# A third seven-product chunk in each feed-forward block, and the turned operand copied out of PSUM by ScalarE

## The chip, the core and the metric

The kernel runs on one core of a Trainium2 chip. The metric is device time in microseconds (us) of one execution: the median of three runs is 1015.85 us (1015.84 to 1016.21). Five engines take part: TensorE (PE in the rows; its weight loads are PEld), VectorE (DVE), ScalarE (ACT), GpSimd (POOL) and SyncE (SP, which issues the weights' transfers). In the trace each engine's own instructions run in the order in which the program lists them, and an instruction that waits holds up those behind it.

## What is computed

Two layers over 256 tokens of width 1024 in float32; each layer is feed-forward, mixer, feed-forward, and every part has a norm ahead of it and one behind it. Cut to what matters here:

```python
def swiglu(x, w_gate, w_up, w_down):
    return (jax.nn.silu(x @ w_gate) * (x @ w_up)) @ w_down

for l in range(2):
    h = swiglu(rms_norm(x, g[0, 0]), ffn_w_gate[l, 0], ffn_w_up[l, 0], ffn_w_down[l, 0])
    x = x + 0.5 * rms_norm(h, g[0, 1])
    ...                       # even_mixer for l = 0, odd_mixer for l = 1
    h = swiglu(rms_norm(x, g[2, 0]), ffn_w_gate[l, 1], ffn_w_up[l, 1], ffn_w_down[l, 1])
    x = x + 0.5 * rms_norm(h, g[2, 1])
```

The gate and up matrices are 1024 x 2816, the down matrix is 2816 x 1024. There are four feed-forward blocks in all.

## The kernel before

**Precision.** A float32 operand is kept as two fp32r tiles, a rounded one (`hi`) and the rest (`lo`), and a product is three matmuls: hi by hi, lo by hi, hi by lo (`mm3`, lines 294 to 296). Of every weight piece of 128 x 1024 ScalarE makes `whi` (line 269) and then VectorE makes `wlo` = raw - whi (line 274). A piece of a gate or up matrix holds two of the eight blocks of 128 rows for 512 columns.

**Buffers.** The raw pieces come over SyncE's queue, 512 KB each, into 13 buffers. The `whi`/`wlo` pairs go through nine buffers in turn (five of one pool and four of another, `RING`), so the cast of a piece can begin only when TensorE is done with the piece nine places before it. `fill` lists pieces up to seven ahead of the matmuls that use them.

**A feed-forward block** takes the 2816 columns in six chunks, `CHUNKS = [512, 512, 512, 256, 512, 512]`, and the two token tiles t = 0, 1. An ordinary chunk of 512 makes gate and up with 8 row blocks x 2 tokens x 2 matrices x 3 = 96 matmuls of 128x512. Then `silu` (ScalarE) and `gated` (VectorE, line 501) make h, which TensorE turns in the next chunk (`turn`, line 403) with a cast and a subtraction behind it (lines 410, 411). The down products of a chunk (48 matmuls for 512 columns) come one chunk later, those of the last two chunks at the block's end.

**A chunk with seven products.** `SEVEN = (2, 4)` names chunks (counted from 0) that are made as a 2x2 block product: the two token tiles by the upper and lower 512 rows on one side, those rows by gate and up on the other. It takes seven block products instead of eight (`seven`, lines 562 to 605), each over four row blocks: 7 x 4 x 3 = 84 matmuls. The price is paid by the other engines: seven pieces of two `whi`/`wlo` pairs instead of four, so 14 casts and 14 subtractions instead of 8 and 8; eight additions of raw pieces on VectorE (line 214); three copies of a PSUM bank to SBUF on ScalarE (`held`, line 572) and three additions on VectorE (`plus`, line 576). The products, in order, go into banks X, W, Y: X, [turn t=0], W, [turn t=1], X again (after the first `held`), Y, X again (after the second), [downs], X again (after the third), W again. The last `plus` needs the end of the last product; then `gated` makes h.

**The sums.** The seven products also need four sums of the token operand's quarters (`row_sums`, lines 523 to 548). Their inputs, the turned x times the norm's weights, are put together again from the `hi` and `lo` halves by four VectorE additions of 128x512 (line 531), and eight more VectorE operations follow.

**The order.** A scheduler in front of the program moves instructions within an engine's list by its own costs and priorities; what it made of the change is shown below.

Of the kernel before, what the change touches and what calls it, by code (L numbers as in the profile page):

```python
# [12 lines left out]
F32 = mybir.dt.float32  # L13
# [3 lines left out]
ALU = mybir.AluOpType  # L17
# [3 lines left out]
P = 128  # L21
# [15 lines left out]
SEVEN = (2, 4)  # L37
# [146 lines left out]
def forward(ctx, tc, a):  # L184
# [211 lines left out]
    def to_T(src, dst, n, j0=0, bank=bank):  # L396

        hi, lo = dst
        for b in range(0, n, 4):
            w = min(4, n - b)  # L400
            ps = bank()
            for i in range(w):
                nc.tensor.transpose(ps[:, i * P:(i + 1) * P], src[:, (b + i) * P:(b + i + 1) * P], ident)  # L403
            done = split(ps[:, :w * P], hi[:, j0 + b:j0 + b + w, :], lo[:, j0 + b:j0 + b + w, :])
        return done
# [7 lines left out]
    def turn_x(t, xg):  # L413

        def half(i):
            return lambda: to_T(xg[:, i * 512:(i + 1) * 512], xT[t], 4, 4 * i, ybank)
        return [half(0), half(1)]
# [35 lines left out]
    def finish(ys, gpost, half, gnext, pieces, at):  # L453


        xg = post_norm(0, ys[0], gpost, half, gnext)
        turns = turn_x(0, xg)
        for i, p in enumerate(pieces):
            if gnext is not None and i in at:
                turns[at.index(i)]()  # L460
            p()
        r0 = rms_x(0) if gnext is not None else None
        xg = post_norm(1, ys[1], gpost, half, gnext)
        if gnext is None:
            return None, None
        return [r0, rms_x(1)], turn_x(1, xg)
# [15 lines left out]
    def ffn(scope, r, turn1, gpost, gnext, at=None):  # L482
        fx, fp, fr = scope
        with fx:
# [38 lines left out]
            def row_sums(fp):  # L523

                xf = [cp.tile([P, D], F32, name="xf", tag="c") for _ in range(NT)]
                A = [[xf[t][:, 512 * i:512 * i + 512] for i in range(2)] for t in range(NT)]
                tt = nc.vector.tensor_tensor
                for t in range(NT):
                    for i in range(2):
                        hi, lo = (v.rearrange("p k n -> p (k n)").bitcast(F32) for v in half(t, i))  # L530
                        tt(A[t][i], hi, lo, op=ALU.add)
# [131 lines left out]
            out = finish(y, gpost, True, gnext, pieces, [n0, n0 + wl // 2])  # L663
# [59 lines left out]
    def mix_out():  # L723
# [21 lines left out]
        def second(gpost, gnext):  # L745
# [4 lines left out]
            return finish(y, gpost, False, gnext, pieces, [8, 10])  # L750
# [492 lines left out]
    def turn_first(t):  # L1243

        def half(i):
            def go():
# [5 lines left out]
                c = cp.tile([P, D], F32, name="c", tag="c")[:, 0:512]  # L1252
# [30 lines left out]
    r, turn1 = ffn(scope, r, turn1, load_g(0, 2, 1), load_g(1, 0, 0))  # L1283
# [34 lines left out]
```

## Time and profile before

| | |
|---|---|
| median of three runs | 1015.85 us |
| the profiled execution, whole | 1009.94 us |
| its span, first to last instruction | 1008.2 us |
| PE busy | 990.5 us (98%) |
| DVE busy | 788.4 us (78%) |
| ACT busy | 583.4 us (58%) |
| weights read | 182.35 MB |
| granted TensorE clock, mean | 1.000 |

The share of busy time is a mean over stretches that differ: where TensorE is never kept waiting, work on the other engines costs nothing, and where it is, the engine that it waits for sets the pace. Matmuls overlap in the pipeline, so that one shows 0.39 us while the next begins 0.227 us later; the pace is read from starts.

### The profile page before, as it was taken

How to read it: one execution, taken by the hardware profiler on the slowest of the kernel's cores; microseconds unless marked ns; L12 is line 12 of the kernel's file. 1: busy time of each engine (PE TensorE's matmuls, PEld its weight loads, DVE VectorE, ACT ScalarE, POOL GpSimd, SP SyncE). 2: the span in 40 equal slices, each digit the busy share in tenths (PEclk: the TensorE clock that was granted, in tenths of full speed). 3: DMA queues.
4: the chain of work that ended last, by engine and by line, in shares of the span. 5: the costliest groups of instructions: out<-in, count | busy, mean ns of one | idle time of the engine just before them, and what ended most of it. 6: DMA issues, size and time to landing. Idle time of an engine off the chain costs nothing.

```text
span 1008.2 us, 13275 instructions
## 1 busy us (share of the span) xinstructions
PE 990.5 (98%) x4883; PEld 825.0 (82%) x4883; DVE 788.4 (78%) x1068; ACT 583.4 (58%) x846; POOL 52.2 (5%) x61
## 2 busy tenths in 40 slices
PE   8999999999999999999999999999999999999997
PEld 6888988888788888888888889888877788889886
DVE  5998996578567899888479988865776779988852
ACT  5746584377644755657447474744665657474731
POOL 1000000021202000000010000000010210000000
PEclk9999999999999999999999999999999999999999
DMA  8938273375223883827456392737634357292701
GB/s 349 374 113 295 70 255 116 105 260 184 99 69 119 312 288 104 305 68 266 175 200 233 113 306 80 271 117 259 230 125 137 119 171 244 95 304 85 252 1 42
DMA packets 51905, 184.26 MB, mean 183 GB/s; under 512 B 6136, under 2 KB 6528, under 8 KB 51840
## 3 DMA queue, kind: packets, MB, share of 16 engines
q1 hardware_dynamic: 48960, 176.05, 50.7%
q10 hardware_dynamic: 2880, 7.37, 2.2%
q8 instruction: 38, 0.62, 0.3%
q14 instruction: 27, 0.22, 0.1%
HBM read 182.35 MB, written 1.05 MB: 182 GB/s over the span
## 4 chain that ended last, share of the span: by engine, by line
PE 89%; DVE 5%; ACT 2%; issue 1%; POOL 1%; DMA 1%; SPq 0%; POOLq 0%; DVEq 0%; ACTq 0%
PE w L294 16%; PE w L296 16%; PE w L295 16%; PE y L294 9%; PE y L296 9%; PE y L295 9%; PE w L342 7%; DVE wlo L274 2%; PE w L403 2%; PE w L1023 1%; ACT whi L269 1%; PE y L403 1%; DMA raw<-in_w_dram 1%; POOL pm L1156 1%; DVE pm L1158 0%
## 5 line engine op out<-in xcount | busy, mean ns | idle before, releaser
L269 ACT CAST whi<-raw 128x1024 fp32r<-128x1024 f32 (+2 forms) x379 | 391.4, 1049 | 268.7 <-PE y L296 90.3
L274 DVE TENSOR_TENSOR wlo<-raw,whi 128x1024 fp32r<-128x1024 f32 (+2 forms) x379 | 456.7, 1228 | 96.1 <-ACT whi L269 92.4
L294 PE MATMUL w<-whi,xThi 128*128 128x512 f32 (+1 forms) x676 | 252.7, 374 | 0.0
L296 PE MATMUL w<-whi,xTlo 128*128 128x512 f32 (+1 forms) x676 | 249.7, 369 | 0.0
L295 PE MATMUL w<-wlo,xThi 128*128 128x512 f32 (+1 forms) x676 | 249.3, 369 | 0.0
L296 PEld LDWEIGHTS w<-whi,xTlo 128*128 128x128 f32 x676 | 127.4, 188 | 21.9 <-issue 0.3
L294 PEld LDWEIGHTS w<-whi,xThi 128*128 128x128 f32 x676 | 127.5, 189 | 21.5 <-issue 1.0
L295 PEld LDWEIGHTS w<-wlo,xThi 128*128 128x128 f32 x676 | 127.5, 189 | 20.4
L294 PE MATMUL y<-whi,hThi 128*128 128x512 f32 x352 | 138.7, 394 | 0.0
L296 PE MATMUL y<-whi,hTlo 128*128 128x512 f32 x352 | 137.5, 391 | 0.0
L295 PE MATMUL y<-wlo,hThi 128*128 128x512 f32 x352 | 137.4, 390 | 0.0
L214 DVE TENSOR_TENSOR raw<-raw 128x1024 f32<-128x1024 f32 x64 | 77.4, 1220 | 1.0
L296 PEld LDWEIGHTS y<-whi,hTlo 128*128 128x128 f32 x352 | 66.1, 188 | 14.3
L295 PEld LDWEIGHTS y<-wlo,hThi 128*128 128x128 f32 x352 | 66.1, 188 | 13.5
L294 PEld LDWEIGHTS y<-whi,hThi 128*128 128x128 f32 x352 | 66.1, 188 | 13.5
L411 DVE TENSOR_TENSOR hTlo<-w,hThi 128x512 fp32r<-128x512 f32 (+1 forms) x48 | 29.8, 641 | 28.4 <-ACT hThi L410 28.0
L438 POOL TENSOR_TENSOR sm<-sm,mhalf 128x1 f32<-128x1 f32 x12 | 6.6, 550 | 701.7 <-DVE sm L436 701.7
L342 PE MATMUL w<-whi,xThi 128*128 128x512 f32 (+2 forms) x124 | 39.0, 393 | 3.9 <-ACT xThi L410 3.9
L410 ACT CAST hThi<-w 128x512 fp32r<-128x512 f32 (+1 forms) x48 | 25.1, 552 | 24.5 <-PE w L403 24.5
L342 PE MATMUL w<-wlo,xThi 128*128 128x512 f32 (+2 forms) x124 | 37.4, 387 | 0.4 <-DVE wlo L274 0.4
L342 PE MATMUL w<-whi,xTlo 128*128 128x512 f32 (+2 forms) x124 | 37.7, 385 | 0.0
L492 ACT ACTIVATE s<-w,sm 128x512 f32<-128x512 f32 (+1 forms) x40 | 25.9, 647 | 15.8 <-PE w L296 15.6
(276 smaller groups left out, 1158.1 us busy)
## 6 DMA issues: line engine op xcount, KB each, us to landing
raw<-in_w_dram SPq DMA_DIRECT2D x325, 512.0 KB, 5.6
g<-in_norm_g_dram ACTq DMA_DIRECT2D x9, 512.0 KB, 5.8
raw<-in_w_dram SPq DMA_DIRECT2D x4, 448.0 KB, 4.1
g<-in_norm_g_dram SPq DMA_DIRECT2D x2, 512.0 KB, 8.5
out_dram<-x SPq DMA_DIRECT2D x4, 256.0 KB, 2.0
E<-in_hw_dram ACTq DMA_DIRECT2D x1, 576.0 KB, 6.8
x<-in_x_dram SPq DMA_DIRECT2D x2, 256.0 KB, 3.1
x<-in_x_dram SPq DMA_DIRECT2D x1, 512.0 KB
```

Source lines behind the costliest of these rows:

```text
L214: nc.vector.tensor_tensor(to, to, what, op=ALU.add)
L269: c = nc.scalar.copy(hi[:, :w], raw[:, :w])
L274: state["lo"] = nc.vector.tensor_tensor(lo[:, :w], raw[:, :w], hi[:, :w].bitcast(F32), op=ALU.subtract)
L294: mm(ps, hi[:, j, :], rhi, start=start, stop=False, skip_group_check=again)
L295: mm(ps, hi[:, j, :], rlo, start=False, stop=False, skip_group_check=again)
L296: state["mm"] = mm(ps, lo[:, j, :], rhi, start=False, stop=stop, skip_group_check=again)
L342: state["mm"] = mm(o, lhs[:, k, :], rhs[:, i, :], start=j == 0 and k == 0, stop=j == 2 and k == KD - 1)
L403: nc.tensor.transpose(ps[:, i * P:(i + 1) * P], src[:, (b + i) * P:(b + i + 1) * P], ident)
L410: c = nc.scalar.copy(h2, ps)
L411: return c, nc.vector.tensor_tensor(lo.rearrange("p a b -> p (a b)"), ps, h2.bitcast(F32), op=ALU.subtract)
L492: nc.scalar.activation(s[:, :w], ps[:, :w], AF.Silu, scale=r[t])
L1023: mm(o, e, e, start=True, stop=True)
```

## The change

`SEVEN` becomes `(2, 4, 5)`: the sixth chunk of each feed-forward block is made with seven products too. No down products stand inside it, since those of the last two chunks come behind it (`kf` and `wp` are 0 there). `to_T` gets a parameter `keep`: with it, after the transposes of x and their `hi` and `lo`, ScalarE copies the PSUM bank over the source tile, so that `row_sums` finds the turned operand there and the four additions go. Two of the four blocks' inputs come from a mixer and one from a feed-forward block, which keep it so; the first block's is kept in SBUF by `turn_first` without a copy. Each half of each token tile is one copy of 128x512: four copies a block in three blocks.

```diff
--- before.py
+++ after.py
@@ -34,7 +34,7 @@
 FIRST_AT = (0, 1)
 BUFS_F = 4
 CHUNKS = [512, 512, 512, 256, 512, 512]
-SEVEN = (2, 4)
+SEVEN = (2, 4, 5)
 RAWS = 8
 RAWS_W = 5
 RING = "wfwfwfwfw"
@@ -393,7 +393,7 @@
         nc.gpsimd.tensor_tensor(r, v, mhalf[:, :n], op=ALU.pow)
         return r
 
-    def to_T(src, dst, n, j0=0, bank=bank):
+    def to_T(src, dst, n, j0=0, bank=bank, keep=False):
 
         hi, lo = dst
         for b in range(0, n, 4):
@@ -402,6 +402,8 @@
             for i in range(w):
                 nc.tensor.transpose(ps[:, i * P:(i + 1) * P], src[:, (b + i) * P:(b + i + 1) * P], ident)
             done = split(ps[:, :w * P], hi[:, j0 + b:j0 + b + w, :], lo[:, j0 + b:j0 + b + w, :])
+            if keep:
+                nc.scalar.copy(src[:, b * P:(b + w) * P], ps[:, :w * P])
         return done
 
     def split(ps, hi, lo):
@@ -410,10 +412,11 @@
             c = nc.scalar.copy(h2, ps)
             return c, nc.vector.tensor_tensor(lo.rearrange("p a b -> p (a b)"), ps, h2.bitcast(F32), op=ALU.subtract)
 
-    def turn_x(t, xg):
+    def turn_x(t, xg, keep):
 
         def half(i):
-            return lambda: to_T(xg[:, i * 512:(i + 1) * 512], xT[t], 4, 4 * i, ybank)
+            return lambda: to_T(xg[:, i * 512:(i + 1) * 512], xT[t], 4, 4 * i, ybank, keep)
+        kept["x", t] = xg
         return [half(0), half(1)]
 
     def rms_x(t, behind=None):
@@ -450,11 +453,11 @@
                     last = nc.vector.tensor_tensor(xg[:, hs], x[t][:, hs], gnext[:, hs], op=ALU.mult)
             return xg
 
-    def finish(ys, gpost, half, gnext, pieces, at):
+    def finish(ys, gpost, half, gnext, pieces, at, keep):
 
 
         xg = post_norm(0, ys[0], gpost, half, gnext)
-        turns = turn_x(0, xg)
+        turns = turn_x(0, xg, keep) if gnext is not None else None
         for i, p in enumerate(pieces):
             if gnext is not None and i in at:
                 turns[at.index(i)]()
@@ -463,7 +466,7 @@
         xg = post_norm(1, ys[1], gpost, half, gnext)
         if gnext is None:
             return None, None
-        return [r0, rms_x(1)], turn_x(1, xg)
+        return [r0, rms_x(1)], turn_x(1, xg, keep)
 
 
     def ffn_scope(block):
@@ -479,7 +482,7 @@
         state["turn"] = state["rawn"] = 0
         return fx, fp, fr
 
-    def ffn(scope, r, turn1, gpost, gnext, at=None):
+    def ffn(scope, r, turn1, gpost, gnext, at=None, keep=False):
         fx, fp, fr = scope
         with fx:
             nch = len(CHUNKS)
@@ -522,13 +525,9 @@
 
             def row_sums(fp):
 
-                xf = [cp.tile([P, D], F32, name="xf", tag="c") for _ in range(NT)]
+                xf = [kept["x", t] for t in range(NT)]
                 A = [[xf[t][:, 512 * i:512 * i + 512] for i in range(2)] for t in range(NT)]
                 tt = nc.vector.tensor_tensor
-                for t in range(NT):
-                    for i in range(2):
-                        hi, lo = (v.rearrange("p k n -> p (k n)").bitcast(F32) for v in half(t, i))
-                        tt(A[t][i], hi, lo, op=ALU.add)
 
                 tt(A[1][1], A[1][1], A[1][0], op=ALU.subtract)
                 tt(A[1][0], A[0][0], A[1][0], op=ALU.subtract)
@@ -660,7 +659,7 @@
             n0 = len(pieces) + wl
             for n in range(2):
                 pieces += [d1(hTl, subs2[i:i + 1], i, (n,), wl - 1) for i in range(wl)]
-            out = finish(y, gpost, True, gnext, pieces, [n0, n0 + wl // 2])
+            out = finish(y, gpost, True, gnext, pieces, [n0, n0 + wl // 2], keep)
             state["pool"] = None
             return out
 
@@ -747,7 +746,7 @@
             part(0, subs[2:], 4, 0)
             part(0, subs[2:], 4, 1)
             pieces = [lambda n=n, i=i: part(1, subs[i:i + 1], 2 + i, n) for n in range(2) for i in range(6)]
-            return finish(y, gpost, False, gnext, pieces, [8, 10])
+            return finish(y, gpost, False, gnext, pieces, [8, 10], True)
 
         return second
 
@@ -1242,6 +1241,8 @@
 
     def turn_first(t):
 
+        kept["x", t] = cp.tile([P, D], F32, name="c", tag="c")
+
         def half(i):
             def go():
                 ps = ybank()
@@ -1249,7 +1250,7 @@
                     turned = nc.tensor.transpose(ps[:, k * P:(k + 1) * P], x[t][:, (4 * i + k) * P:(4 * i + k + 1) * P], ident)
                     if t == 1 and k == 0:
                         after(turned, state["mm"])
-                c = cp.tile([P, D], F32, name="c", tag="c")[:, 0:512]
+                c = kept["x", t][:, 512 * i:512 * i + 512]
                 with tc.high_priority():
                     m = nc.vector.tensor_tensor(c.rearrange("p (k n) -> p k n", k=4), ps.rearrange("p (k n) -> p k n", k=4), gT[:, 4 * i:4 * i + 4].unsqueeze(2).broadcast_to([P, 4, P]), op=ALU.mult)
                 if t == 1:
@@ -1280,7 +1281,7 @@
         second = even(r, turn1, tabm, lb, lbm)
     scope = ffn_scope(2)
     r, turn1 = second(gpost, gnext)
-    r, turn1 = ffn(scope, r, turn1, load_g(0, 2, 1), load_g(1, 0, 0))
+    r, turn1 = ffn(scope, r, turn1, load_g(0, 2, 1), load_g(1, 0, 0), keep=True)
     r, turn1 = ffn(ffn_scope(3), r, turn1, load_g(1, 0, 1), load_g(1, 1, 0))
     gpost, gnext = load_g(1, 1, 1), load_g(1, 2, 0)
     second = odd(r, turn1, tabd)
```

The places below are in the third feed-forward block (the first of layer 1). `raw`, `whi`, `wlo` are pieces of weights, `u` are the held products, `w` and `y` PSUM banks, `h` the gated result.

**VectorE, from the `plus` of the fifth chunk's first product sum to its two `gated`.** Before:

```order
L576 TENSOR_TENSOR u_5963<-w_5823,u_5963 128x512
L274 TENSOR_TENSOR wlo_5975<-raw_5972,whi_5974 128x1024
L274 TENSOR_TENSOR wlo_5995<-raw_5992,whi_5994 128x1024
L274 TENSOR_TENSOR wlo_6001<-raw_5998,whi_6000 128x1024
L274 TENSOR_TENSOR wlo_6026<-raw_6023,whi_6025 128x1024
L576 TENSOR_TENSOR u_5902<-w_5823,u_5902 128x512
L274 TENSOR_TENSOR wlo_6032<-raw_6029,whi_6031 128x1024
L501 SCALAR_TENSOR_TENSOR h_6017<-u_5902,sm_4845,s_5905 128x512
L501 SCALAR_TENSOR_TENSOR h_6019<-u_5963,sm_4846,s_5990 128x512
```

Now, the last twelve rows up to the same two `gated` (ahead of them stand the same `plus` and two more L214):

```order
L214 TENSOR_TENSOR raw_6010<-raw_6010,raw_6038 128x1024
L274 TENSOR_TENSOR wlo_6014<-raw_5971,whi_6013 128x1024
L274 TENSOR_TENSOR wlo_6021<-raw_5977,whi_6020 128x1024
L214 TENSOR_TENSOR raw_5971<-raw_5971,raw_6038 128x1024
L214 TENSOR_TENSOR raw_5977<-raw_5977,raw_6045 128x1024
L214 TENSOR_TENSOR raw_6017<-raw_6017,raw_6045 128x1024
L274 TENSOR_TENSOR wlo_6042<-raw_5971,whi_6041 128x1024
L274 TENSOR_TENSOR wlo_6049<-raw_5977,whi_6048 128x1024
L575 TENSOR_TENSOR u_5946<-w_5867,u_5946 128x512
L274 TENSOR_TENSOR wlo_6073<-raw_6070,whi_6072 128x1024
L504 SCALAR_TENSOR_TENSOR h_6065<-u_5946,sm_4893,s_5949 128x512
L504 SCALAR_TENSOR_TENSOR h_6067<-u_6007,sm_4894,s_6036 128x512
```

The two `gated` (L501, now L504) give the h that TensorE turns inside the sixth chunk. Before, five `wlo` stood between the first `plus` and the first of them; now six additions of raw pieces and five `wlo` do.

**ScalarE, inside the sixth chunk.** Before, its second half:

```order
L269 CAST whi_6025<-raw_6023 128x1024
L269 CAST whi_6031<-raw_6029 128x1024
L269 CAST whi_6061<-raw_6059 128x1024
L269 CAST whi_6067<-raw_6065 128x1024
L269 CAST whi_6121<-raw_6119 128x1024
L269 CAST whi_6127<-raw_6125 128x1024
L492 ACTIVATE s_6095<-w_6021,sm_4802 128x512
L492 ACTIVATE s_6097<-w_6022,sm_4823 128x512
L410 CAST hThi_6099<-w_6101 128x512
L410 CAST hThi_6108<-w_6110 128x512
```

Now, from the second `held` of that chunk to the third:

```order
L571 COPY u_6180<-w_6069 128x512
L269 CAST whi_6138<-raw_6070 128x1024
L269 CAST whi_6143<-raw_6076 128x1024
L269 CAST whi_6160<-raw_6038 128x1024
L269 CAST whi_6164<-raw_6045 128x1024
L269 CAST whi_6187<-raw_6185 128x1024
L269 CAST whi_6193<-raw_6191 128x1024
L269 CAST whi_6214<-raw_6212 128x1024
L495 ACTIVATE s_6183<-u_6126,sm_4850 128x512
L269 CAST whi_6220<-raw_6218 128x1024
L571 COPY u_6209<-w_6069 128x512
```

Seven casts, a `silu` and an eighth cast stand between two copies of the same PSUM bank, `w_6069` (X). Before, no bank was copied in this chunk.

**TensorE, at the same place.** Before, from the last product of the sixth chunk into the downs:

```order
L294 MATMUL w_6118<-whi_6031,xThi1_93 128x512
L295 MATMUL w_6118<-wlo_6032,xThi1_93 128x512
L296 MATMUL w_6118<-whi_6031,xTlo1_94 128x512
L294 MATMUL y_5015<-whi_6061,hThi_6099 128x512
L295 MATMUL y_5015<-wlo_6062,hThi_6099 128x512
L296 MATMUL y_5015<-whi_6061,hTlo_6100 128x512
```

Now, behind the product that the third `held` copies:

```order
L296 MATMUL w_6069<-whi_6110,Slo0_5078 128x512
L294 MATMUL y_5065<-whi_6187,hThi_6094 128x512
L294 MATMUL y_5066<-whi_6187,hThi_6094 128x512
L294 MATMUL y_5067<-whi_6187,hThi_6128 128x512
L294 MATMUL y_5068<-whi_6187,hThi_6128 128x512
L295 MATMUL y_5065<-wlo_6188,hThi_6094 128x512
L296 MATMUL y_5065<-whi_6187,hTlo_6095 128x512
L295 MATMUL y_5066<-wlo_6188,hThi_6094 128x512
L296 MATMUL y_5066<-whi_6187,hTlo_6095 128x512
L294 MATMUL y_5065<-whi_6193,hThi_6094 128x512
L294 MATMUL y_5066<-whi_6193,hThi_6094 128x512
L294 MATMUL w_6069<-whi_6138,xThi1_93 128x512
```

Ten down products of the block's end have been moved ahead of the next product into bank X (`w_6069`).

## Rows read from the trace of the kernel before

**Rows 1.** The page: span, engines, granted clock, chain that ended last.

```profile
span 1008.2 us, 13275 instructions
...
PE 990.5 (98%) x4883; PEld 825.0 (82%) x4883; DVE 788.4 (78%) x1068; ACT 583.4 (58%) x846; POOL 52.2 (5%) x61
...
PEclk9999999999999999999999999999999999999999
...
PE 89%; DVE 5%; ACT 2%; issue 1%; POOL 1%; DMA 1%; SPq 0%; POOLq 0%; DVEq 0%; ACTq 0%
```

**Rows 2.** Waits of PE: for whom, us in total, times, longest us.

```profile
PE w L342 <- ACT xThi L410: 3.9, 2, 2.9
```

**Rows 3.** Groups by form: busy us, mean ns of one | idle before, releasers.

```profile
L274 DVE TENSOR_TENSOR wlo<-raw,whi 128x1024 fp32r<-128x1024 f32 x373 | 450.7, 1231 | 94.1 <-ACT whi L269 90.6
L269 ACT CAST whi<-raw 128x1024 fp32r<-128x1024 f32 x373 | 386.3, 1052 | 263.5 <-PE w L296 87.5 <-PE y L296 86.8 <-DVE raw L214 29.7
...
L214 DVE TENSOR_TENSOR raw<-raw 128x1024 f32<-128x1024 f32 x64 | 77.4, 1220 | 1.0
...
L572 ACT COPY u<-w 128x512 f32<-128x512 f32 x24 | 14.0, 582 | 5.8 <-PE w L296 5.8
...
L501 DVE SCALAR_TENSOR_TENSOR h<-u,sm,s 128x512 f32<-128x512 f32 x16 | 11.3, 745 | 0.0
L531 DVE TENSOR_TENSOR xf<-xThi,xTlo 128x512 f32<-128x512 f32 x16 | 10.5, 685 | 0.0
```

**Rows 4.** Timeline of PE, sixth chunk of the third block: start us, us, what.

```profile
655.69 0.39 PE L294 MATMUL w<-whi,xThi 128*128 128x512 f32 x1
...
658.41 0.39 PE L294 MATMUL w<-whi,xThi 128*128 128x512 f32 x1
```

**Rows 5.** The chain in time order, turn in that chunk: start us, us, what.

```profile
666.74 0.87 PE w L403 x8
```

**Rows 6.** Stretches of the fifth and sixth chunk: length, busy us by engine, clock, DMA.

```profile
631.00:655.70 24.70, 24.70 (x113) 20.37 (x112) 20.18 (x20) 19.53 (x23) 0.00 (x0) 1.00 0.78 269
655.70:678.40 22.70, 22.70 (x106) 18.89 (x105) 14.54 (x16) 10.73 (x13) 0.00 (x0) 1.00 0.35 117
```

**Rows 7.** Timeline of ACT, third block.

```profile
640.05 2.00 ACT L269 CAST whi<-raw 128x1024 fp32r<-128x1024 f32 x2
642.33 1.06 ACT L269 CAST whi<-raw 128x1024 fp32r<-128x1024 f32 x1 [0.28 <-ACT whi L269]
643.65 1.06 ACT L269 CAST whi<-raw 128x1024 fp32r<-128x1024 f32 x1 [0.26 <-PE w L296]
644.61 0.72 ACT L492 ACTIVATE s<-u,sm 128x512 f32<-128x512 f32 x1
```

**Rows 8.** Timeline of DVE, third block.

```profile
643.41 0.68 DVE L576 TENSOR_TENSOR u<-w,u 128x512 f32<-128x512 f32 x1
644.01 3.52 DVE L274 TENSOR_TENSOR wlo<-raw,whi 128x1024 fp32r<-128x1024 f32 x3
647.45 0.68 DVE L576 TENSOR_TENSOR u<-w,u 128x512 f32<-128x512 f32 x1
...
655.97 0.68 DVE L576 TENSOR_TENSOR u<-w,u 128x512 f32<-128x512 f32 x1
```

**Rows 9.** Timeline of DVE, first block, ahead of its fifth chunk and at its end.

```profile
90.83 1.23 DVE L274 TENSOR_TENSOR wlo<-raw,whi 128x1024 fp32r<-128x1024 f32 x1 [1.58 <-ACT whi L269]
...
144.06 0.68 DVE L576 TENSOR_TENSOR u<-w,u 128x512 f32<-128x512 f32 x1
```

**Rows 10.** Timeline of PE, first block, start of its sixth chunk.

```profile
149.40 0.39 PE L294 MATMUL w<-whi,xThi 128*128 128x512 f32 x1
```

**Rows 11.** Stretch at the third block's start: busy us by engine.

```profile
520.00:535.00 15.00, 15.00 (x71) 12.18 (x70) 12.84 (x21) 10.13 (x15) 1.48 (x2) 1.00 0.50 163
```

## The prediction

> **What bounds the kernel now.** I read the page first: TensorE is busy for 98% of the span, the clock is granted in full in all 40 slices, and 89% of the chain that ended last is TensorE [rows 1]. Then the waits of TensorE, where the reader is to see that they are short: the longest line is 3.9 us in all, in two waits for x's cast [rows 2]. In the fifth and sixth chunk of the third block TensorE is busy for the whole of both stretches [rows 6]. There its pace is the time, and a matmul taken out there is worth its 0.227 us: twelve of them go from 655.69 to 658.41, 2.72 us [rows 4]. Last I compared those two stretches, which the average over the span hides: in the fifth (seven products) VectorE works 20.2 and ScalarE 19.5 of 24.7 us, in the sixth (ordinary) 14.5 and 10.7 of 22.7 [rows 6]. The sixth is where those two engines get their lead back.
>
> **What goes.** 96 - 84 = 12 matmuls of the sixth chunk in each of four blocks: 4 x 2.72 = 10.9 us, all on the path as long as TensorE is fed. Transposes and down products stay as many. Of `row_sums` 16 additions of 685 ns go, 11 us of VectorE [rows 3]; they stand where TensorE waits for nobody, so I count them as 0. Could their going help later? In the first block, where VectorE's lead at the sixth chunk is smallest, it could be 4 x 685 ns = 2.7 us; but between there and the fifth chunk VectorE waits for `whi`, once for 1.58 us [rows 9], so that being earlier only makes it wait longer. I take 0, with 2.7 as the bound. For such a move the Trainium skill (Perfetto Trace Analysis, Optimizing Scalar/DVE Operations) says that it may make sense to give work to ScalarE where VectorE is saturated. Here VectorE works 12.8 of 15 us around the block's start [rows 11], without TensorE waiting for it, so by the row the move is worth nothing.
>
> **What comes, off TensorE.** In each block: six more casts on ScalarE (1052 ns each), six more subtractions (1231 ns), eight additions of raw pieces (1220 ns), three copies (582 ns) and three `plus` (0.60 us from one start to the next) [rows 3, 8]. So inside the sixth chunk VectorE has 14 x 1.15 + 8 x 1.22 + 3 x 0.60 + 2 x 0.745 for `gated` + 2 x 0.6 for the turned h = 30 us of work, against 84 x 0.227 + 0.9 for the turns [rows 5] = 20 us of TensorE. An excess of 10 us can only come out of the lead. The lead is bounded by the nine `whi`/`wlo` buffers: the first two casts of the sixth chunk wait, today too, for TensorE to give a buffer back and start at 642.33 and 643.65 [rows 7], so VectorE cannot begin the sixth chunk before 644.01 [rows 8], 11.7 us ahead of TensorE. Where the order makes something late I walk through the third block by its new order.
>
> **The first wait: the turned h.** TensorE turns the fifth chunk's h after only one product of the sixth, at 655.69 + 2.72 = 658.4. On VectorE h stands behind: two `wlo` (from 644.01; 3.44 us for three, so to 646.3), a `plus` (0.6), six additions (7.3), four `wlo` (4.6), which makes 658.8, then the second `plus` (0.6), one `wlo` (1.15) and `gated` (0.745): 661.3. The last product of the fifth chunk, which the second `plus` needs, is long done (today that `plus` runs at 655.97 [rows 8]), so VectorE's queue decides. TensorE waits 661.3 - 658.4, about 2.8 us. Nothing else stands ahead of the turn in its list. Bounds: 0, if VectorE had nothing in front (655.97 + 0.6 + 0.745 = 657.3), and 3.5 if every operation took its full 1.23 us. I take 2.8, since all durations are from rows. Behind the turn queue W's first product and everything after it.
>
> **The second wait: the third copy of X.** From 661.3: two turns (0.5 each), three products to the end of X's second use (661.3 + 0.5 + 2.7 + 0.5 + 2.7 = 667.8), then Y (670.5) and X again (673.2). The next product adds into X, so it waits until ScalarE has copied X the third time. ScalarE does the second copy from 667.9 to 668.4 and then, by the new order, seven casts at 1.0 us (two take 2.00 [rows 7]), a `silu` of 0.72, another cast and the third copy of 0.58: 677.7. In an ordinary fifth chunk down products stand in that place. So 4.5 us of TensorE, of which the ten down products that were moved there fill 10 x 0.227 = 2.3; they need `wlo` of the first down piece, which VectorE reaches at about 675.9, just in time. Net 2.2 us. Bounds: 0 (a copy directly behind its product, about 1 us, lies under the ten) and 4.5 (the ten can't run there). I take 2.2. After it, `gated` of the sixth chunk has 14 down products (3.2 us) in front of its turn, enough for `plus`, `wlo` and `gated` (2.5 us), and the lead of the next block is set by the norm at this block's end, as now.
>
> **The first block.** There VectorE reaches the same `plus` at 144.06, 5.3 us ahead of the sixth chunk at 149.40 [rows 9, 10], not 9.4 as in the third block (646.3 against 655.69). Its order differs a little: five additions, four `wlo` and two `plus` stand ahead of h, 144.06 + 6.1 + 4.6 + 1.2 + 0.745 = 156.7, against 149.40 + 2.72 = 152.1: a wait of 4.6 us. The copies of X come 0.5 and 3.0 us late there (the casts ahead of the third are fewer, but wait for VectorE's additions), and three down products fill 0.7. Net of the 2.72 saved: 4.6 + 0.5 + 2.3 - 2.7, with 0.1 lost in the turns, +4.7.
>
> **Copies for the sums.** Twelve copies of 582 ns in three blocks, between other work of ScalarE, which is busy 10.1 of 15 us there [rows 11]. In the list they come behind the casts that TensorE waits for, or in the time in which ScalarE waits for the next transposes. I take 0; the bound is all twelve on the path, 7 us, below 0 nothing, since they only add.
>
> **Sum.** Third block: -2.7 + 2.8 + 2.2, and 0.1 for the turns that stand apart: +2.4. The second and the fourth have the same lists. 3 x 2.4 + 4.7 = +11.9. The profiled execution of 1009.94 us (its span 1008.2 and 1.7 around it) becomes about 1021.8; it lay 5.9 us below the median of the runs, so the median of 1015.85 becomes 1027.7, and I say 1027.5.
>
> **Rivals.**
> *TensorE stays fed* (faster): the lead holds and all of 10.9 us shows: 1005. For it: TensorE is the busiest engine and its waits are nearly nil [rows 1, 2]. Against it: VectorE's 30 us against 20, and the place of h in its list. The Trainium skill (Perfetto Trace Analysis, Identifying the Most-Contended Engine) would have the engine with the highest occupancy made faster first; by that rule alone 1005 is the result, and its next section warns that the engine that binds changes between stretches, as rows 6 show here. Chance 0.08.
> *Only one wait stays* (no change): if VectorE or ScalarE has 2 to 3 us more lead than I count, for one because an addition overlaps its neighbours more than in the fifth chunk, one of the waits goes and the other cancels the gain: 1015 to 1018. Chance 0.08.
> *The copies for the sums land on the path*: from the point where ScalarE is late with x's casts, up to 12 x 0.58 = 7 us more: 1034. For it: x's cast is the one thing that TensorE waits for at a block's start [rows 2]. Against: their place in the list. Chance 0.07.
> *The clock falls* in the new waits. TensorE's longest idle time here is the 2.9 us at the kernel's start, with the full clock granted around it [rows 1, 2]; the first block's wait would be 4.6 us. At half speed for one product behind each of eight waits: 8 x 2.7 = 22 us, 1049. The Trainium skill (TensorE: Matmul & The Clock Gate, Part 1: The HAM clock gate) says that an idle TensorE falls back to the half clock; no row here shows a fall. Chance 0.05.
>
> **How the numbers follow.** My forecast has 0.72 and spreads over 1020 to 1033, by the bounds of the two waits around the values taken. What a measurement of this kernel can tell from no change is about 0.2%, 2 us. Slower by more: 0.72 + 0.07 + 0.05 and a quarter of the second rival, 0.86; the same: 0.06; faster: 0.08. The range of 1017 to 1034 leaves out the fed TensorE, the fallen clock and some tails.
>
> **What would show it.** In the third block's trace: a wait of TensorE before the first turn of the sixth chunk that a `gated` of VectorE ends, 2 to 3 us in three blocks and over 4 in the first; six additions of raw pieces ahead of that `gated`; a wait ahead of the product behind the third copy that ScalarE ends, with down products in it; 48 matmuls fewer; no wait in `row_sums`. I am wrong if TensorE's idle time has not grown by 15 us or more, or if the added waits sit elsewhere.

## The result, and the profile after

The changed kernel takes 1024.56 us (median of six runs, 1021.53 to 1026.9) against 1015.45 us for six runs of the kernel before: a ratio of 1.0096, 95% interval 1.0075 to 1.0117. It is slower by about 1%, inside the range, 2.9 us under the time predicted. Its profiled execution is 1024.73 us, where the sum said 1021.8. So the two errors have opposite signs, and both are told below.

The page of the kernel after: span, busy time, granted clock in 40 slices, chain that ended last (against [rows 1]).

```profile
span 1022.6 us, 13290 instructions
...
PE 989.2 (97%) x4835; PEld 819.3 (80%) x4835; DVE 847.6 (83%) x1120; ACT 616.4 (60%) x894; POOL 52.4 (5%) x61
...
PEclk9999998999999999999999999999999999999999
...
PE 76%; DVE 12%; issue 5%; ACT 3%; DMA 3%; POOL 1%; DVEq 0%; SPq 0%; POOLq 0%; ACTq 0%
```

There are 48 matmuls fewer, as said, and yet the span is 14.4 us longer. VectorE's share of the chain went from 5% to 12%, and one slice of the clock is below full. Waits of TensorE after (for whom, us in all, times, longest), against [rows 2]:

```profile
PE w L403 <- DVE h L504: 10.6, 4, 4.0
PE y L295 <- DVE wlo L274: 4.2, 3, 1.4
```

The first line is the first wait of the prediction, in all four blocks. The second is a wait inside the ten down products that were moved into the second wait. VectorE after, third block, from the second `plus` of the fifth chunk to its two `gated` (start us, us, what):

```profile
656.43 0.68 DVE L575 TENSOR_TENSOR u<-w,u 128x512 f32<-128x512 f32 x1
657.03 3.49 DVE L214 TENSOR_TENSOR raw<-raw 128x1024 f32<-128x1024 f32 x3
660.43 2.36 DVE L274 TENSOR_TENSOR wlo<-raw,whi 128x1024 fp32r<-128x1024 f32 x2
662.71 3.49 DVE L214 TENSOR_TENSOR raw<-raw 128x1024 f32<-128x1024 f32 x3
666.11 2.35 DVE L274 TENSOR_TENSOR wlo<-raw,whi 128x1024 fp32r<-128x1024 f32 x2
668.38 0.68 DVE L575 TENSOR_TENSOR u<-w,u 128x512 f32<-128x512 f32 x1
668.99 1.21 DVE L274 TENSOR_TENSOR wlo<-raw,whi 128x1024 fp32r<-128x1024 f32 x1
670.12 1.41 DVE L504 SCALAR_TENSOR_TENSOR h<-u,sm,s 128x512 f32<-128x512 f32 x2
```

No gap stands between these rows: VectorE is a full queue for 14.4 us, and h is ready only at 670.87. TensorE over the same sixth chunk: its first matmul, the turn of h, the last matmul ahead of the second wait, the moved down products, and the next product into X.

```profile
665.84 0.39 PE L294 MATMUL w<-whi,xThi 128*128 128x512 f32 x1
...
670.91 0.66 PE L403 MATMUL w<-ident,h 128*128 128x128 f32 x4 [2.19 <-DVE h L504]
...
682.59 0.39 PE L296 MATMUL w<-whi,Slo 128*128 128x512 f32 x1
682.97 1.20 PE L294 MATMUL y<-whi,hThi 128*128 128x512 f32 x4
685.56 0.50 PE L295 MATMUL y<-wlo,hThi 128*128 128x512 f32 x1 [1.40 <-DVE wlo L274]
...
687.08 0.40 PE L294 MATMUL w<-whi,xThi 128*128 128x512 f32 x1
```

And ScalarE between the second and the third copy of X:

```profile
677.58 0.59 ACT L571 COPY u<-w 128x512 f32<-128x512 f32 x1 [2.19 <-PE w L296]
678.06 6.75 ACT L269 CAST whi<-raw 128x1024 fp32r<-128x1024 f32 x7
684.70 0.74 ACT L495 ACTIVATE s<-u,sm 128x512 f32<-128x512 f32 x1
685.32 1.05 ACT L269 CAST whi<-raw 128x1024 fp32r<-128x1024 f32 x1
686.26 0.59 ACT L571 COPY u<-w 128x512 f32<-128x512 f32 x1
```

TensorE waits 2.19 us at the turn. At the second wait it issues ten matmuls from 682.82 to 687.08, 2.27 us of work, so 2.0 us are lost. Two chains end there together: the row names `wlo` on VectorE, but the copy of X lands at 686.85 and would have held the product behind anyway. VectorE just ahead of it:

```profile
676.04 2.35 DVE L214 TENSOR_TENSOR raw<-raw 128x1024 f32<-128x1024 f32 x2
679.14 4.63 DVE L274 TENSOR_TENSOR wlo<-raw,whi 128x1024 fp32r<-128x1024 f32 x4 [0.75 <-ACT whi L269]
683.69 0.68 DVE L575 TENSOR_TENSOR u<-w,u 128x512 f32<-128x512 f32 x1
684.29 3.48 DVE L274 TENSOR_TENSOR wlo<-raw,whi 128x1024 fp32r<-128x1024 f32 x3
```

Here VectorE's queue has a gap of 0.75 us, until ScalarE has made the first cast behind the second copy. That cast needs the first of the two additions, which ends at 677.26; but it stands behind the copy, which waits for a product of TensorE until 677.58. So 0.75 of the 1.40 us is the order of ScalarE's list. The rest is VectorE's: four `wlo` and a `plus` stand ahead of the `wlo` that the down product needs.

Three stretches show TensorE's clock at half, which no slice of [rows 1] does (length, busy us of PE, PEld, DVE, ACT, POOL, granted clock):

```profile
154.10:160.90 6.80, 4.82 (x14) 3.95 (x15) 6.80 (x9) 1.59 (x3) 0.00 (x0) 0.50 0.00 0
256.50:259.90 3.40, 3.40 (x12) 2.83 (x11) 1.14 (x3) 2.14 (x4) 0.00 (x0) 0.50 0.37 146
485.20:488.60 3.40, 3.40 (x10) 2.82 (x11) 3.38 (x4) 1.15 (x2) 0.00 (x0) 0.50 0.00 0
```

0.50 is 1.2 of 2.4 GHz. The first and the third lie at the wait for h of the first and the second block; the one in the middle is in the first mixer. Half the working time in them is lost: 2.4, 1.7 and 1.7 us.

Where the 14.4 us lie, from the starts of TensorE's first turn of x behind each block (for the third block 516.45 to 698.34 before, 526.06 to 710.30 after): first block +4.6 (2.4 of it clock), first mixer +1.7 (all clock), second block +3.4 (1.7 clock), third +2.3 (0.5 of it at its start, where the second token's x is turned), second mixer +0.8 (0.56 of it a wait for x), last block +1.7.

### The profile page after: what moved, and what is told of

Read it like the earlier page. It is cut to its first block, busy times and chain, and to the rows that moved or that the text cites. A ratio compares the mean times of both kernels' runs of the same rounds, so it can differ in the third digit from the quotient of the medians.

```text
span 1022.6 us, 13290 instructions
## 1 busy us (share of the span) xinstructions
PE 989.2 (97%) x4835; PEld 819.3 (80%) x4835; DVE 847.6 (83%) x1120; ACT 616.4 (60%) x894; POOL 52.4 (5%) x61
## 2 busy tenths in 40 slices
DMA packets 51905, 184.26 MB, mean 180 GB/s; under 512 B 6136, under 2 KB 6528, under 8 KB 51840
## 4 chain that ended last, share of the span: by engine, by line
PE 76%; DVE 12%; issue 5%; ACT 3%; DMA 3%; POOL 1%; DVEq 0%; SPq 0%; POOLq 0%; ACTq 0%
PE w L294 13%; PE w L295 13%; PE w L296 13%; PE y L295 8%; PE y L296 7%; PE y L294 7%; PE w L342 6%; DVE wlo L274 6%; PE w L403 2%; ACT whi L269 2%; DMA raw<-in_w_dram 2%; DVE raw L214 2%; PE w L1022 1%; DMA lp<-in_od_lambda_dram 1%; DVE x L447 1%
## 5 line engine op out<-in xcount | busy, mean ns | idle before, releaser
L269 ACT CAST whi<-raw 128x1024 fp32r<-128x1024 f32 (+1 forms) x403 | 413.3, 1049 | 229.8 <-PE y L296 86.2
L274 DVE TENSOR_TENSOR wlo<-raw,whi 128x1024 fp32r<-128x1024 f32 (+1 forms) x403 | 483.5, 1228 | 66.1 <-ACT whi L269 62.2
L294 PE MATMUL w<-whi,xThi 128*128 128x512 f32 (+1 forms) x596 | 221.9, 373 | 0.0
L296 PE MATMUL w<-whi,xTlo 128*128 128x512 f32 (+1 forms) x596 | 218.9, 367 | 0.0
L295 PE MATMUL w<-wlo,xThi 128*128 128x512 f32 (+1 forms) x596 | 218.8, 367 | 0.0
L296 PEld LDWEIGHTS w<-whi,xTlo 128*128 128x128 f32 x596 | 112.7, 189 | 18.9 <-issue 0.3
L214 DVE TENSOR_TENSOR raw<-raw 128x1024 f32<-128x1024 f32 x96 | 114.9, 1222 | 1.0
L294 PE MATMUL w<-whi,oThi 128*128 128x512 f32 x96 | 41.1, 428 | 0.0
L296 PE MATMUL w<-whi,oTlo 128*128 128x512 f32 x96 | 38.9, 405 | 0.0
L295 PE MATMUL w<-wlo,oThi 128*128 128x512 f32 x96 | 38.7, 403 | 0.0
```

Source lines behind the costliest of these rows:

```text
L214: nc.vector.tensor_tensor(to, to, what, op=ALU.add)
L269: c = nc.scalar.copy(hi[:, :w], raw[:, :w])
L274: state["lo"] = nc.vector.tensor_tensor(lo[:, :w], raw[:, :w], hi[:, :w].bitcast(F32), op=ALU.subtract)
L294: mm(ps, hi[:, j, :], rhi, start=start, stop=False, skip_group_check=again)
L295: mm(ps, hi[:, j, :], rlo, start=False, stop=False, skip_group_check=again)
L296: state["mm"] = mm(ps, lo[:, j, :], rhi, start=False, stop=stop, skip_group_check=again)
```

## The experiments

Ratios are to the kernel before on the same chip, 95% intervals behind them. The medians of the kernel before differ from one set of runs to another (1015.45 beside the changed kernel, 1011.0 to 1012.5 in the experiments), so only ratios are compared.

**1. The two halves of the change, each alone.** First, `SEVEN` back:

```diff
-SEVEN = (2, 4, 5)
+SEVEN = (2, 4)
```

> Only the second half of the change: the turned operand copied from PSUM by ScalarE, chunks 3 and 5 with seven products as before (sixth chunk ordinary). Theory (the wait sits in the sixth chunk's VectorE and ScalarE lists; the copies and the vanished additions are hidden): as before, 1015.4 within 2 us, no new wait of TensorE, granted clock about 1.000. Rival (copies for the sums land on the path of x's casts): up to 7 us more, 1022. Rival (the vanished 11 us of VectorE work pays): 1008 to 1013.

Measured 1.0008 (0.9994 to 1.0022). The copies for the sums cost nothing, and the 16 vanished additions bring nothing. No wait is new.

Second, the kernel before with only the line `SEVEN = (2, 4, 5)` of the change:

> Only the first half of the change: sixth chunk with seven products, the sums' inputs put together by VectorE's four additions as before. Theory: as the whole change, 1024.5 within 2 us, with TensorE's waits for h of 4.0 us in the first block and 2.2 us in the others. Rival (copies cost): 1018. Rival (vanished additions had paid part): 1027 or more, above all in the first block, whose wait for h would be up to 2.7 us longer (6.7 us).

Measured 1.0138 (1.0119 to 1.0156), with the same waits:

```profile
PE w L403 <- DVE h L501: 10.5, 4, 3.9
PE y L295 <- DVE wlo L274: 4.2, 3, 1.4
```

So the whole loss comes from the sixth chunk. That it lies 0.4% above the whole change is not explained by a wait: the third block's turn of h is followed by half clock here, which it is not in the whole change, and the two were measured in different sets of runs. The difference stays open.

**2. The turn of h later in TensorE's list.**

```diff
-                hT = [turn(0, CHUNKS[ci - 1]), None]
...
                 prod(Y, half(0, 1), True)
                 u2 = held(X)
                 s0 = silu(0, plus(p1, Y), 512)
+                hT = [turn(0, CHUNKS[ci - 1]), None]
                 prod(X, S3, False)
+                hT[1] = turn(1, CHUNKS[ci - 1])
```

> The whole change, but inside the sixth chunk the turn of the fifth chunk's h stands later in TensorE's list: token 0 behind the product into Y, token 1 behind the third product into X. Theory: the wait for h (2.2 us three times, 4.0 once, 10.6 us in all) goes, and with it the half clock seen behind the first and the second of them (6.8 and 3.4 us at half speed, about 5 us lost); the lead that VectorE lacks comes back in part at the wait for the third copy and the first down piece (1.4 us each so far, to 2.5): 1013 to 1017. Rival (the wait only moves, because VectorE's total work sets the chunk's end): 1021 to 1025, with waits of 3 us or more at the down products.

Measured 1.0102 (1.0084 to 1.0119): no gain. The wait for h fell to 0.9 us in all, and this came in its place:

```profile
PE y L294 <- ACT whi L269: 7.8, 4, 2.0
```

In the third block the idle time of the two waits shrank from 3.6 to 2.2 us, but 3.4 us at half clock follow the wait now (683.9 to 687.3), and the block lasts 184.17 us against 184.24. The rival is nearer: the wait taken away at the turn is collected at the chunk's end. VectorE's list makes h as late as before, and the chunk's first copy of X still waits for it on ScalarE (1.19 us; `u` has two buffers).

**3. The wait filled with matmuls that nobody needs.**

```diff
                 prod(X, half(0, 0), True)
+                W = bank()
+                if ci == nch - 1:
+                    for _ in range(10):
+                        mm(W, S1[0][:, 0, :], xhi_512, start=True, stop=True)
                 hT = [turn(0, CHUNKS[ci - 1]), None]
-                W = bank()
                 prod(W, S1, True)
```

> The whole change, with ten matmuls of 128x512 whose result is thrown away (10 x 0.227 = 2.27 us a block) in the sixth chunk between the first product and the turn of h, where TensorE waits 2.2 us (4.0 in the first block). Theory (the wait costs its own length and, by the half clock granted behind it, about as much again in some blocks): the idle time goes in three blocks at no cost, about 1.7 us stay in the first, and the clock stays full there; ratio 1.003 to 1.007 against the whole change's 1.0096. Rival (the clock falls for another reason than the wait): half clock at the same places, 1.009 to 1.012. Rival (the ten matmuls add to the wait): 1.015 or more.

Measured 1.0136 (1.0116 to 1.0155), which neither theory gave (`xhi_512` in the diff is 512 columns of the turned x; the diff shows the ten matmuls without the lines that fix their order). What it shows is local: in the second block the wait is gone and the clock stays full (the stretch that had 0.50 before),

```profile
485.30:489.30 4.00, 4.00 (x19) 3.34 (x18) 4.00 (x5) 3.45 (x4) 0.00 (x0) 1.00 0.00 0
```

and that block is 1.0 us shorter than in the whole change (184.36 against 185.41); the waits at the down pieces stay (1.40 each), and the third block is as long as before (184.26). Half clock stood elsewhere instead, 6.8 us of it in the first mixer, where the kernel is unchanged. Where the clock falls differs from run to run, so for its share the run is inconclusive.

**4. VectorE's additions in the sixth chunk left out.**

```diff
     def add(to, what):
-        nc.vector.tensor_tensor(to, to, what, op=ALU.add)
+        if not state["skip"]:            # set for the sixth chunk's sums
+            nc.vector.tensor_tensor(to, to, what, op=ALU.add)
```

> The whole change, but VectorE's eight additions of raw weight pieces in the sixth chunk are left out of the computation (four blocks, 32 additions of 1.22 us); everything else stays. Theory: without 9.8 us of VectorE work in the chunk the wait for h goes in every block, and of the waits at the third copy at most 1 us stays: the saving of 10.9 us shows, 1004 to 1009. Rival (ScalarE's list, in which seven casts and a silu stand ahead of the third copy, sets the second wait by itself): the wait for h goes but 1.4 us or more stay at the copy in each block, 1010 to 1014. Rival (the added waits are not VectorE's): 1020 or more.

Measured 0.9919 (0.9904 to 0.9935), 8 us faster than the kernel before. One wait for h is left, 0.5 us in the first block, and none at the copies or the down pieces. In the third block VectorE now even waits for casts ahead of h, three times between 645 and 653 us. So the first wait is paid by VectorE's additions: six of them are 7.0 of the 14.4 us in which VectorE's queue runs without a gap up to h. For the second wait the run does not decide, because the order changed too: between the second and third copy ScalarE has four casts here instead of eight, and four more stand between the first copy and the second, where the whole change has none. In the whole change 0.75 of that wait's 1.40 us is ScalarE's order, by the rows above. The same gap and the same wait stand in the third block of the first kernel of experiment 5, although TensorE waits 4.84 us for h there:

```profile
697.39 4.63 DVE L274 TENSOR_TENSOR wlo<-raw,whi 128x1024 fp32r<-128x1024 f32 x4 [0.75 <-ACT whi L269]
```

```profile
703.81 0.50 PE L295 MATMUL y<-wlo,hThi 128*128 128x512 f32 x1 [1.40 <-DVE wlo L274]
```

A kernel with all the additions and another order of ScalarE's casts was not run.

**5. Additions moved to GpSimd**, which works 5% of the span: those of one sum, then of two, in every chunk of seven products.

```diff
-                    raw = add(kept["B12", k], kept["B22", k])
+                    raw = add(kept["B12", k], kept["B22", k], nc.gpsimd)
```

> The whole change, with the two additions that make the third weight sum (T3) in every chunk with seven products moved from VectorE to GpSimd (24 of 96). Theory (VectorE's excess in the sixth chunk sets both waits; leaving out all eight additions took both away): 2.4 us less of VectorE, so the wait for h goes in three blocks and falls to about 1.5 us in the first, what stays is at the down pieces; ratio to the kernel before 0.996 to 1.003 (the whole change stood at 1.0096). Rival (an addition of 128x1024 on GpSimd, at least twice the 1.2 to 1.7 us that its additions of 128x512 take here, comes too late for the cast behind it): a new wait for whi of 1 us or more in each of twelve chunks, 1.010 or more.

> The whole change, with the additions of the third and the fourth weight sum (T3, T4) on GpSimd in every chunk with seven products (48 of 96). Theory: 4.9 us less of VectorE in each of these chunks, no wait for h, at most small ones at the down pieces: ratio 0.989 to 0.995, near the kernel without the additions (0.992). Rival (GpSimd's four additions in a row, some 10 to 13 us, are late for the casts of T4): a wait for whi in each chunk, 1.000 to 1.010.

Measured 1.0329 (1.0309 to 1.0349) and 1.0329 (1.0308 to 1.0349). Both expectations failed, and the rivals' reason too: TensorE waits mainly for h, 21.1 and 20.4 us in all, and not for a cast. The group of VectorE's own additions and that of GpSimd's, in the first of the two kernels:

```profile
L214 DVE TENSOR_TENSOR raw<-raw 128x1024 f32<-128x1024 f32 x72 | 106.5, 1495 | 1.1
L214 POOL TENSOR_TENSOR raw<-raw 128x1024 f32<-128x1024 f32 x24 | 74.1, 3096 | 429.9 <-DVE raw L214 214.9 <-DMA raw<-in_w_dram 169.8 <-DVE n L685 45.2
```

and in its third block what VectorE and GpSimd do at the same time:

```profile
673.06 6.70 DVE L274 TENSOR_TENSOR wlo<-raw,whi 128x1024 fp32r<-128x1024 f32 x2
```

```profile
672.07 6.60 POOL L214 TENSOR_TENSOR raw<-raw 128x1024 f32<-128x1024 f32 x2 [28.69 <-DMA raw<-in_w_dram]
```

Two subtractions that take 2.36 us alone take 6.70 beside two additions on GpSimd. VectorE's busy time rose from 847.6 to 868.1 us with 24 additions (29 us) fewer: the rest was stretched by 50 us, two thirds of GpSimd's 74. The Trainium skill (Perfetto Trace Analysis, Optimizing Scalar/DVE Operations) warns that GpSimd and VectorE share a read port, so that moving work between them may not help. The trace agrees that it does not, at 2.3% more time here; that the port is the reason no run here shows.

**6. Where the three chunks stand.** Same matmuls, casts and additions, another order of widths and of `SEVEN`. First, none behind another:

```diff
-CHUNKS = [512, 512, 512, 256, 512, 512]
-SEVEN = (2, 4, 5)
+CHUNKS = [512, 512, 256, 512, 512, 512]
+SEVEN = (1, 3, 5)
```

> The same three chunks' worth of seven products, but none behind another: widths 512, 512, 256, 512, 512, 512 with seven products in the second, fourth and sixth chunk, so that an ordinary chunk stands between. Same matmuls, casts and additions as the whole change. Theory, if it is the fifth chunk in front that takes VectorE's lead away: wait for h under 1 us, ratio 0.993 to 0.999. Rival (the lead is bounded by the nine weight buffers anyway, so the sixth chunk alone overdraws it): the waits stay at 2 us or more a block, 1.004 to 1.010. Second rival (the second chunk stands directly behind the sums' 12 VectorE operations and waits there instead): a new wait early in each block, 1.005 or more.

Measured 1.0126 (1.0107 to 1.0146). The sixth chunk has no wait over 0.4 us in any block, as the theory had it; the second rival took the gain, with waits in the second chunk (of the first and of the third block):

```profile
62.26 0.97 PE L294 MATMUL y<-whi,hThi 128*128 128x512 f32 x3 [2.15 <-ACT whi L269]
...
561.22 0.49 PE L296 MATMUL w<-whi,oTlo 128*128 128x512 f32 x1 [1.55 <-DVE oTlo L545]
```

Then third, fourth and sixth, with the narrow chunk fifth (`regain`) or second (`regain_tight`); `regain` also has the first turn at the block's end behind both of token 0's first down pieces:

```diff
+CHUNKS = [512, 512, 512, 512, 256, 512]      # regain
+CHUNKS = [512, 256, 512, 512, 512, 512]      # regain_tight
+SEVEN = (2, 3, 5)                            # both
```

> The whole change, but the order of chunks is 512, 512, 512, 512, 256, 512 with seven products in the third, fourth and sixth (the same number of matmuls of each kind per block; the first turn at the block's end stands behind both of token 0's first down pieces). Theory (the lead is capped by the nine weight buffers, about 11.7 us, and a chunk may overdraw it by no more): third and fourth chunk hold 48 down products each, so VectorE has 35 us of work against 31 of TensorE, an excess of 4 each, 8 together; the narrow chunk gives 11 back; the sixth takes 10. No wait over 0.5 us inside the chunks: ratio 0.990 to 0.996, with up to 1 us a block lost at the block's end, where fewer down products cover the norm. Rival (the additions ahead of h in VectorE's list make the wait whatever the lead): waits for h of 2 us stay, 1.003 to 1.010.

> As the run before, with the narrow chunk second: 512, 256, 512, 512, 512, 512, seven products in the third, fourth and sixth, nothing else changed. Theory: the third chunk holds only 24 down products, so VectorE's excess is 7 us there and 4 in the fourth, 11 together, just the lead; an ordinary chunk gives 16 back ahead of the sixth. Waits of 0 to 1.5 us in the fourth chunk, none in the sixth: ratio 0.991 to 0.999. Rival (as above): 1.003 to 1.010, with the wait in the sixth chunk.

Measured 1.0022 (1.0011 to 1.0034) and 1.0050 (1.0033 to 1.0066). `regain` has no wait for h among its listed waits. Its last three blocks are shorter than before, by 1.4, 1.0 and 2.2 us (the third: 523.05 to 703.94, 180.89 us against 181.89), though TensorE waits up to 1.28 us at the end of the third. So the expected 0.990 to 0.996 is missed: the first block takes it all back, with a wait of 1.6 us, the one below and 6.8 us at half clock around the end of the latter:

```profile
129.95 0.80 PE L294 MATMUL w<-whi,xThi 128*128 128x512 f32 x1 [4.49 <-ACT u L571]
```

`regain_tight` waits for h in the fourth chunk (2.1, 2.2, 1.1 and 2.2 us), more than the 1.5 expected, and not in the sixth. So the wait moves with the chunks' places and does not belong to the sixth chunk as such.

**7. One more pair of weight buffers**, paid with two raw buffers.

```diff
-AHEAD_F = 6        -BUFS_F = 4        -RAWS = 8        -RING = "wfwfwfwfw"
+AHEAD_F = 7        +BUFS_F = 5        +RAWS = 6        +RING = "wfwfwfwfwf"
```

> The whole change with ten pairs of weight buffers instead of nine, listed eight pieces ahead instead of seven, and to make room eleven raw buffers instead of thirteen. Theory (the lead's cap): one more piece of lead is about 1.2 us, so the wait for h falls from 2.2 to about 1 us in three blocks and from 4.0 to 2.8 in the first, and the wait at the down pieces to under 0.7: ratio 1.001 to 1.006. Rival (raw buffers limit the additions, so two fewer cost more than the pair brings): 1.010 or more, with waits for transfers or for additions.

Measured 1.0121 (1.0102 to 1.0140): the waits for h stay at 2.05 to 2.26 us in three blocks, and in the first a wait of 3.6 us for a cast at the down pieces stands in their place. Since two raw buffers went at the same time, it does not tell which buffers cap the lead. That the nine pairs do is not shown.

**8. The order of `regain` in the last three blocks, the first block as before.**

```diff
+CHUNKS_FIRST, SEVEN_FIRST = [512, 512, 512, 256, 512, 512], (2, 4)
+CHUNKS_REST, SEVEN_REST = [512, 512, 512, 512, 256, 512], (2, 3, 5)
...
+        CHUNKS, SEVEN = (CHUNKS_FIRST, SEVEN_FIRST) if state["block"] == 0 else (CHUNKS_REST, SEVEN_REST)
```

> The order of chunks of the regain run (seven products in the third, fourth and sixth, the narrow chunk fifth) in the last three feed-forward blocks; the first block as in the kernel before (two chunks with seven products). Theory (where VectorE is given its lead back ahead of the sixth chunk the saving shows, and the first block, whose lead is smaller, can't pay): the first block as before; second, third and last 1.4, 1.0 and 2.2 us shorter, as in the regain run: 4.6 us, ratio 0.994 to 0.997. Rival (the regain run's waits in the first block only move to the second when the first is relieved): 1.000 to 1.003.

Measured 0.9950 (0.9932 to 0.9967): 1007.14 us against 1011.81 us, faster than both kernels. Its page:

```profile
span 1005.3 us, 13268 instructions
...
PE 984.1 (98%) x4847; PEld 816.8 (81%) x4847; DVE 830.7 (83%) x1103; ACT 607.7 (60%) x885; POOL 51.9 (5%) x61
```

No wait for h or for a copy is in it. The first block ends at 192.9 us (192.64 before); the other three are 1.4, 1.8 and 2.2 us shorter. Of the 8.2 us that the three chunks could save, 5.4 show in the blocks; a wait for x at the third block's end (0.49 us) is part of the rest. The span is shorter by 2.9 us only, because the two mixers take 1.2 and 1.1 us back, 0.84 of it another wait for x; the cause of the rest is open.

Additions ahead of h make no wait by themselves. In the fourth chunk of this kernel's third block, which follows another one with seven products, five of them stand between the second `plus` and the two `gated`:

```profile
593.50 0.69 DVE L577 TENSOR_TENSOR u<-w,u 128x512 f32<-128x512 f32 x1
...
605.01 1.41 DVE L506 SCALAR_TENSOR_TENSOR h<-u,sm,s 128x512 f32<-128x512 f32 x2
```

```profile
607.19 0.39 PE L295 MATMUL w<-whi,xThi 128*128 128x512 f32 x1
...
609.91 0.60 PE L404 MATMUL w<-ident,h 128*128 128x128 f32 x4
```

That `plus` stands 13.7 us ahead of the chunk, not 9.4 as in the changed kernel, and h is ready 4.2 us before its turn. The lists differ in more than the lead, and a kernel with the `gated` ahead of the additions was not run.

## Why the prediction came out right, and where it did not

**The gain and the first wait.** TensorE reaches the turn 2.7 us into the chunk, as said. VectorE's second `plus` stands 9.4 us ahead of the chunk (656.43 against 665.84), the very lead taken from [rows 7, 8]. From there to h it takes 14.4 us where I had 15.0, so the wait is 2.2 and not 2.8; 3.96 and not 4.6 in the first block. Experiment 4 shows that the additions make it. The bound on the lead is less sure than I wrote: of the two casts that I had waiting for TensorE, [rows 7] put only the one at 643.65 down to it, and that the nine buffers set the lead is not shown (experiment 7).

**The second wait** was put at 2.2 us net and is 2.0. Its cause was half told: I had the third copy of X as the hold and the down pieces' `wlo` as just in time; the row names the `wlo`, with the copy 1.3 us behind it, so the sign that I gave (a wait that ScalarE ends) did not come. What both start from, eight casts behind the second copy in ScalarE's list, is what the prediction walked through; that VectorE's additions alone make this wait is not shown. TensorE's idle time, span less busy time, grew from 17.7 to 33.4 us, just past the 15 that I had named.

**A block**: +2.4 said for the third; 2.2 + 2.0 - 2.7 with 0.1 for the turns is +1.6, and the second and the last block measure +1.7 without the clock. The third measures +2.3. Of the rest 0.5 us lies ahead of its fifth chunk, which begins 114.79 us into the block against 114.25 before; that term was missing, and its cause stays open (with the copies alone the block is as long as before, 181.99 us). The first block was said at +4.7. It measures +4.6, but 2.4 of this is clock: the copies, put at 2.8 us there (0.5 and 2.3 net), cost about 0.9 (2.2 - 3.96 + 2.72 - 0.1).

**The sums and the copies for them**, both 0: confirmed by experiment 1, where they stand alone. With it falls the rival that the copies land on the path; the fed TensorE and the single wait fall with the two waits above.

**What failed.** First, the clock. It was a rival at 1049 with a chance of 0.05, half speed behind all eight waits. It fell in part: behind two of eight waits, and once in a mixer, 5.8 us in the profiled run. A cost that comes in parts should have been a term with a range. Second, the step from the profiled execution to the median. I added 5.9 us, by which the kernel before stood above its own profiled run. That run had the full clock throughout; in the experiments, runs of that kernel at a granted clock of 0.999 to 1.000 took 1010.2 to 1011.8 us, and those at 0.991 took 1014.6 to 1015.8. That is only part of it, since at 0.995 they lie anywhere from 1010.0 to 1016.3. The changed kernel's runs stood at 0.989 to 0.993, its profiled one among them, and its median is within 0.2 us of the profiled time. Without the offset and with the clock the sum is 1021.8 + 5.8 - 2.5 (first block) = 1025.1, against 1024.73 measured. The forecast of the median was good because the missing clock and the offset cancel, and that was luck.

## What to carry to other kernels

Count a faster matmul scheme per stage as a debt on the engine that feeds it: here each such chunk saves TensorE 2.7 us and costs VectorE some 18 us of work, which has to be earned back in a cheaper stage in front. Moving the resulting wait only shifted where it was collected, and filling it gained nothing over the whole kernel. Before dropping such a change, try its place: with a stage to recover in front of the sixth chunk the time went from 1.0096 to 1.0022 of the time before, and to 0.995 when the first block, which has less lead, was left as it was. And see whether a profiled run had the full clock before its distance from the median is carried over to another kernel.

## What the runs showed of the hardware

The same wait of 2.2 us was followed by half clock in the second block and by full clock in the third and the last:

```profile
670.90:674.90 4.00, 3.98 (x22) 3.39 (x23) 4.00 (x5) 1.27 (x3) 0.00 (x0) 1.00 0.01 2
974.40:978.40 4.00, 4.00 (x22) 3.42 (x23) 4.00 (x5) 1.33 (x3) 0.00 (x0) 1.00 0.01 4
```

So the same wait was followed by a slower TensorE in one of three places: its cost is a chance and not a fixed price. The Trainium skill (TensorE: Matmul & The Clock Gate, Part 1: The HAM clock gate) says that the clock follows how busy TensorE has lately been. In these rows the length of the wait alone does not tell which way it goes.

In many profiled runs the clock also stood at half from about 8.5 to 15 us, while the first weights arrive (a mean of 0.56 over 8.50 to 15.30 in the kernel of experiment 8, with TensorE busy for 4.96 of 6.8 us; 1.00 before). That kernel's first block ended at 192.9 us. In the first run of experiment 1, which makes that block the same way and had the full clock there, it ended at 192.0. So the slow clock cost about 0.9 us at most in this place.
